# Low parts of twelve weight units made by an adding DMA instead of a subtraction

## The chip, the cores and the metric

The program runs on one core of a Trainium2 chip. The metric is the device time of one execution in microseconds (us), as the median of several runs. The engines are named as the profile names them: PE is the matrix engine (TensorE), PEld its weight loads, DVE is VectorE, ACT is ScalarE, POOL is GpSimd, and SP is the engine that issues most DMAs.

## The reference

Two model blocks run one after the other on a sequence of 512 tokens of width 1024, all in float32. Only the first mixer of the first block is touched:

```python
def even_mixer(h, w_in, sink, w_pool, pool_scale, w_out):
    z = h @ w_in
    q, k, v, u = jnp.split(z, [A_WIDTH, A_WIDTH + A_KV_WIDTH, A_WIDTH + 2 * A_KV_WIDTH], axis=-1)
    q = rope(q.reshape(Bsz, S, A_HEADS, A_HEAD_DIM))      # 8 heads of 64
    k = rope(k.reshape(Bsz, S, A_KV_HEADS, A_HEAD_DIM))
    ya = windowed_gqa(q, k, v, sink)
    yb = multiscale_pool(u, w_pool, pool_scale)           # 4 groups, windows 2, 4, 8, 16
    return jnp.concatenate([ya, yb], axis=-1) @ w_out
```

After it come a squared-ReLU MLP, a second mixer, a second MLP, and a second block. Nothing of them changes.

## The kernel before, in words

Every float32 product is made of three faster ones. An activation or a weight `w` is split into a high part `hi`, which is `w` rounded to the short format that PE multiplies fast, and a low part `lo = w - hi`. For each 128x128 block of weights PE then issues three multiplies of 512 columns, in this order: `hi` of the activation by `wh` (the weight's high part), `hi` by `wl` (its low part), and `lo` by `wh`. In the trace they are `mm<-hi,wh`, `mm<-hi,wl`, `mm<-lo,wh`.

Weights come in units of 128x1024 elements, 512 KB, which are eight such blocks, so 24 multiplies. A unit is loaded by a DMA of SP into a tile `wr`. `copy` (line 572) writes `wh`, on ACT or POOL, whichever the planner expects to be free first, and `tt` (line 586) makes `wl` from `wr` and `wh`, on DVE or POOL by the same rule. There are four buffers each for `wr`, `wh` and `wl`.

The program for all engines is written by a planner that runs when the kernel is built. `_Flow` keeps a clock of its own (`fl.now`), adds a cost for each instruction, and lets tasks go on when they are due. So a changed cost or a changed due time moves the order of the instructions on every engine. Each engine then executes its own list strictly in order and waits at an instruction until what it needs is there. The rule that matters below: the planner puts the multiplies of a unit on PE's list only when `Unit.ready` says that the unit is there, at the planner's clock.

The stage around the change is phase "a", the first mixer. PE's list mixes two sorts of work there. One is the attention of eight heads: score products (`sc`), transposes of the weights of the softmax (`tr`), and the products with the values (`av`), each in turn with maxima (`mx`, `nm`) and low parts (`pl`) on DVE and exponentials (`p<-sc,nm`), scalings (`p<-p,w`), high parts (`ph`) and sums of halves (`cmb`) on ACT. The other sort is filling work that depends on no attention: the projections of `pooling()` from units `ein3` and `ein4` (two each), then the first half of the output projection, units `eout0` and `eout1` (two each). After the attention the second half, `eout2` and `eout3`, follows. These are the last twelve units of the first mixer.

Each of the four projections of `pooling()` feeds a chain, `pool_chain`: `up` is read out of PSUM by DVE, window sums `us` are added up on DVE or POOL (one addition for the first group, four for the last), `pd` is made on DVE, its high part on ACT, its low part `lo<-pd,hi` on DVE or POOL, and then PE multiplies by the unit `wpool`, again as three multiplies.

Of the kernel before, what the change touches and what calls it, by code (L numbers as in the profile page):

```python
# [13 lines left out]
AF = mybir.ActivationFunctionType  # L14
ALU = mybir.AluOpType
# [41 lines left out]
_WT = {}  # L57
# [431 lines left out]
def tile_hybrid(ctx: ExitStack, tc: tile.TileContext, wt, xT, pT, prm_d, cst_d, out):  # L489
    nc = tc.nc  # L490
# [3 lines left out]
    fl = _Flow()  # L494
    go = fl.go
    V, S, G = (_Engine(fl, e, k) for e, k in ((nc.vector, "V"), (nc.scalar, "S"), (nc.gpsimd, "G")))
# [13 lines left out]
    def uid(s):  # L510
        cnt[0] += 1
        return f"{s}{cnt[0]}"
# [44 lines left out]
    def f(ap):  # L557
        return ap.bitcast(F32)
# [12 lines left out]
    def first(*engines):  # L571

        return min(engines, key=lambda e: max(e[0].free, fl.now) + e[1])[0]

    def width(ap):
        n = 1
        for d in ap.shape[1:]:
            n *= d
        return n

    def copy(out, src, scale=None):

        n, ps = width(out), src.space == PSUM
        sc = 1.0 if scale is None else scale
        e = first((S, 0.06 + n / 1090.0), *(() if ps else ((G, 0.07 + n * 0.00117 + fl.gc),)))
        if e is S:
            S.activation(out, src, AF.Copy, scale=sc)
        else:
            G.tensor_scalar(out, src, sc, 1.0, op0=ALU.mult, op1=ALU.mult)

    def tt(op, out, a, b, bias=None):

        n = width(out)
        if PSUM in (a.space, b.space):
            e = V
        else:
            e = first((V, 0.07 + n / 960.0), (G, 0.07 + n * 0.00227 + (fl.gt if bias is None else bias)))
        e.tensor_tensor(out, a, b, op=op)


    NRAW, NSPLIT, AHEAD = 4, 4, 3
    units, order = {}, []

    class Unit:
# [57 lines left out]
        def split(self):  # L662
            while len(self.at) < len(self.parts):
                self.load()
            r = self.raw
            self.hi = wp.tile([P, 1024], F32R, tag="whi", bufs=NSPLIT, name=uid("wh"))
            self.lo = wp.tile([P, 1024], F32R, tag="wlo", bufs=NSPLIT, name=uid("wl"))
            wl["split"] += 1
            wl["due"] -= 1
            for (c0, c1), t in zip(self.parts, self.at):  # L670
                while fl.now < t:
                    yield 0.1
                copy(self.hi[:, c0:c1], r[:, c0:c1])
                yield
                tt(ALU.subtract, self.lo[:, c0:c1], r[:, c0:c1], f(self.hi[:, c0:c1]), fl.gw)
                if c1 == self.n:
                    wl["raw"] -= 1
                yield
                self.ready = c1

        def use(self, n):
# [4 lines left out]
    wl = {"raw": 0, "split": 0, "dma": 0.8, "due": 0}  # L686
# [1729 lines left out]
```

## Time and profile before

| what | value |
|---|---|
| median of three runs | 1477.36 us (1476.55 to 1479.11) |
| the profiled execution | 1479.96 us |
| its span in the profile | 1478.2 us |
| PE busy in that span | 1449.5 us |
| DVE, ACT, POOL busy | 899.0, 649.5, 310.7 us |

The profiled execution is 1.8 us longer than its span, which is what lies before its first and behind its last instruction, and 2.6 us longer than the median of the runs. A share of busy time over the whole span says little about one stage; the stage of the first mixer lies in the first 150 us.

### The profile page before, as it was taken

To read this page: it belongs to the slowest core of one execution; us is meant where nothing else is said; L and a number is where in the kernel's file an instruction comes from. 1 tells how busy PE (TensorE), PEld (TensorE's weight loads), DVE (VectorE), ACT (ScalarE), POOL (GpSimd) and SP (SyncE) were. 2 spreads that over 40 slices of the span, in tenths; PEclk is the share of its full clock that TensorE was granted. 3 is DMA by queue.
4 is the path that set the end of the run, shared out by engine and by line. 5 is a ranking of instruction groups with operands and counts; after the bars stand their busy time and mean duration, and the time that the engine had idled before them with its cause. 6 is when DMAs were issued, how large, how long until landed. Compare 5 with 4: busy or idle time off the path is not lost.

```text
span 1478.2 us, 18891 instructions
## 1 busy us (share of the span) xinstructions
PE 1449.5 (98%) x6789; PEld 1174.4 (79%) x6789; DVE 899.0 (61%) x1410; ACT 649.5 (44%) x1192; POOL 310.7 (21%) x291
## 2 busy tenths in 40 slices
PE   8999999999999999899999999999999999999998
PEld 5777878888888888688888888888787788888787
DVE  7896864655434555977775665657755566536413
ACT  5684432433222347487433434334521576324623
POOL 5451220211102013631120210202110000100332
PEclk9999999999999999999999999999999999999999
DMA  6113588888423454333499999999865223346252
GB/s 212 52 44 99 176 291 272 286 290 280 133 95 100 137 213 158 127 129 128 149 318 330 327 330 330 314 336 323 287 216 195 109 86 115 115 182 214 103 196 89
DMA packets 118317, 291.44 MB, mean 197 GB/s; under 512 B 13136, under 2 KB 14672, under 8 KB 118224
## 3 DMA queue, kind: packets, MB, share of 16 engines
q1 hardware_dynamic: 118080, 289.98, 57.9%
q8 instruction: 53, 0.87, 0.2%
q14 instruction: 40, 0.33, 0.1%
q10 hardware_dynamic: 144, 0.26, 0.1%
HBM read 205.26 MB, written 84.93 MB: 196 GB/s over the span
## 4 chain that ended last, share of the span: by engine, by line
PE 83%; DMA 7%; DVE 5%; issue 1%; ACT 1%; SPq 1%; POOL 0%; DVEq 0%; POOLq 0%; ACTq 0%
PE mm L561 72%; PE sc L561 4%; PE av L561 3%; PE tr L565 3%; DMA kr<-in_wt_dram 3%; DMA wk<-klo 2%; PE tr L561 1%; DMA wk<-khi 1%; DVE wl L363 1%; DMA x<-in_xT_dram 1%; ACT wh L363 1%; DVE klo L363 0%; DVE gz L363 0%; DVE sg L363 0%; DMA pin<-in_pT_dram 0%
## 5 line engine op out<-in xcount | busy, mean ns | idle before, releaser
L561 PE MATMUL mm<-hi,wh 128*128 128x512 f32 (+1 forms) x1276 | 509.4, 399 | 0.8 <-POOL wh L363 0.5
L561 PE MATMUL mm<-hi,wl 128*128 128x512 f32 (+1 forms) x1276 | 501.1, 393 | 4.4 <-DVE wl L363 2.6
L561 PE MATMUL mm<-lo,wh 128*128 128x512 f32 (+1 forms) x1276 | 499.3, 391 | 0.3 <-POOL lo L363 0.3
L561 PEld LDWEIGHTS mm<-lo,wh 128*128 128x128 f32 x1276 | 240.4, 188 | 55.6 <-POOL lo L363 0.8
L561 PEld LDWEIGHTS mm<-hi,wl 128*128 128x128 f32 x1276 | 240.8, 189 | 54.9 <-DVE wl L363 3.6
L561 PEld LDWEIGHTS mm<-hi,wh 128*128 128x128 f32 x1276 | 240.9, 189 | 52.9 <-ACT wh L363 1.5
L363 ACT ACTIVATE khi<-kr 128x512 fp32r<-128x512 f32 x120 | 75.8, 632 | 308.8 <-DMA kr<-in_wt_dram 303.1
L561 PE MATMUL mm<-ul,wh 128*128 128x512 f32 x512 | 201.6, 394 | 1.8 <-DVE ul L363 1.8
L561 PE MATMUL mm<-uh,wh 128*128 128x512 f32 x512 | 201.7, 394 | 0.3 <-ACT uh L363 0.3
L561 PE MATMUL mm<-uh,wl 128*128 128x512 f32 x512 | 201.6, 394 | 0.0
L363 DVE TENSOR_TENSOR wl<-wr,wh 128x1024 fp32r<-128x1024 f32 (+1 forms) x145 | 184.5, 1273 | 6.4 <-ACT wh L363 4.8
L363 DVE TENSOR_TENSOR klo<-kr,khi 128x512 fp32r<-128x512 f32 x150 | 124.3, 830 | 87.7 <-ACT khi L363 77.3
L363 ACT ACTIVATE wh<-wr 128x1024 fp32r<-128x1024 f32 (+1 forms) x147 | 148.8, 1013 | 47.8 <-PE mm L561 34.4
L363 DVE TENSOR_TENSOR x<-x,mm 128x512 f32<-128x512 f32 x112 | 76.8, 686 | 151.0 <-PE mm L561 146.3
L363 POOL TENSOR_TENSOR ma<-ma 128x512 f32<-128x512 f32 x62 | 85.4, 1377 | 282.7 <-ACT uh L363 232.2
L561 PEld LDWEIGHTS mm<-ul,wh 128*128 128x128 f32 x512 | 96.2, 188 | 25.2 <-DVE ul L363 2.9
L561 PEld LDWEIGHTS mm<-uh,wh 128*128 128x128 f32 x512 | 96.1, 188 | 23.1 <-ACT uh L363 0.7
L561 PEld LDWEIGHTS mm<-uh,wl 128*128 128x128 f32 x512 | 96.2, 188 | 22.3
L363 ACT ACTIVATE p<-sc,nm 128x512 f32<-128x512 f32 (+3 forms) x136 | 75.2, 557 | 30.4 <-DVE nm L363 27.3
L363 DVE TENSOR_TENSOR pl<-tr,ph 128x512 fp32r<-128x512 f32 (+2 forms) x108 | 66.5, 623 | 25.4 <-ACT ph L363 24.8
L363 POOL TENSOR_SCALAR khi<-kr 128x512 fp32r<-128x512 f32 x30 | 28.6, 953 | 250.3 <-DMA kr<-in_wt_dram 214.1
L363 DVE SCALAR_TENSOR_TENSOR ma<-mm,rb 128x512 f32<-128x512 f32 x64 | 44.1, 688 | 52.4 <-PE mm L561 52.2
(290 smaller groups left out, 1619.0 us busy)
## 6 DMA issues: line engine op xcount, KB each, us to landing
wr<-in_wt_dram SPq DMA_DIRECT2D x144, 512.0 KB, 5.3
kr<-in_wt_dram SPq DMA_DIRECT2D x150, 256.0 KB, 5.9
wk<-khi SPq DMA_DIRECT2D x150, 256.0 KB, 5.9
wk<-klo SPq DMA_DIRECT2D x150, 256.0 KB, 5.7
wh<-wk SPq DMA_DIRECT2D x74, 512.0 KB, 3.3
wl<-wk SPq DMA_DIRECT2D x74, 512.0 KB, 4.2
x<-xs SPq DMA_DIRECT2D x16, 256.0 KB, 5.1
cst<-in_cst_dram SPq DMA_DIRECT2D x8, 256.0 KB, 5.4
```

Source lines behind the costliest of these rows:

```text
L363: return fn(*a, **k)
L561: PE.matmul(o, l, r, start=start, stop=stop, skip_group_check=True)
L565: PE.transpose(o, i, idn)
```

## The change

For the units named in `ADDED`, all of the twelve, the low part is made in another way. ACT writes the negated, rounded weight into the tile `wl` (the negated high part). `copy` writes `wh` as before. Then POOL issues a DMA that reads the float32 weights from HBM once more and adds them onto what is in `wl`. The subtraction goes away. The planner counts the `wr` buffer as free as soon as the copies are made; it books 1 us of POOL for the issue and 3 us of DMA time, and takes the unit as ready at least 7 us after the issue.

```diff
+    ADDED = ("ein3", "ein4", "eout0", "eout1", "eout2", "eout3")
@@ class Unit, split
-                copy(self.hi[:, c0:c1], r[:, c0:c1])
-                yield
-                tt(ALU.subtract, self.lo[:, c0:c1], r[:, c0:c1], f(self.hi[:, c0:c1]), fl.gw)
-                if c1 == self.n:
-                    wl["raw"] -= 1
-                yield
+                if self.name in ADDED:
+
+                    S.activation(self.lo[:, c0:c1], r[:, c0:c1], AF.Copy, scale=-1.0)
+                    copy(self.hi[:, c0:c1], r[:, c0:c1])
+                    if c1 == self.n:
+                        wl["raw"] -= 1
+                    yield
+                    c = 1024 * self.i
+                    nc.gpsimd.dma_start(self.lo[:, c0:c1], wt[_WT[self.name], :, c + c0:c + c1], accum_op=ALU.add)
+                    G.free = max(G.free, fl.now) + 1.0
+                    wl["dma"] = max(wl["dma"], fl.now) + 3.0
+                    yield max(7.0, wl["dma"] + 4.0 - fl.now)
+                else:
+                    copy(self.hi[:, c0:c1], r[:, c0:c1])
+                    yield
+                    tt(ALU.subtract, self.lo[:, c0:c1], r[:, c0:c1], f(self.hi[:, c0:c1]), fl.gw)
+                    if c1 == self.n:
+                        wl["raw"] -= 1
+                    yield
```

The lists of the engines are the same as before, names of buffers apart, up to the first of these units and again behind the first mixer. In between they differ. On PE, in the middle of the attention, where the fifth head is applied (`av_1019` before, `av_1028` after), multiplies of the last pooling projection stood between the attention's products:

```order
L561 MATMUL av_1019<-ph_997,v_367 128x256
L561 MATMUL av_1019<-pl_998,v_367 128x384
L561 MATMUL mm_970<-hi_173,wh_975 128x512
L561 MATMUL mm_970<-hi_173,wl_976 128x512
L561 MATMUL mm_970<-lo_174,wh_975 128x512
L561 MATMUL mm_970<-hi_189,wh_975 128x512
L561 MATMUL mm_970<-hi_189,wl_976 128x512
L561 MATMUL mm_970<-lo_190,wh_975 128x512
L561 MATMUL mm_970<-hi_196,wh_975 128x512
L561 MATMUL mm_970<-hi_196,wl_976 128x512
```

And at the same place of the attention now:

```order
L561 MATMUL av_1028<-ph_995,v_367 128x384
L561 MATMUL av_1028<-pl_996,v_367 128x384
L565 MATMUL tr_1065<-cst,p_882 128x128
L565 MATMUL tr_1065<-cst,p_904 128x128
L565 MATMUL tr_1065<-cst,p_925 128x128
L565 MATMUL tr_1065<-cst,p_882 128x128
L565 MATMUL tr_1077<-cst,p_904 128x128
L565 MATMUL tr_1077<-cst,p_925 128x128
L565 MATMUL tr_1077<-cst,p_882 128x128
L561 MATMUL av_1028<-ph_1030,v_367 128x256
L561 MATMUL av_1028<-pl_1031,v_367 128x256
```

The multiplies have moved behind this piece of attention, because the planner takes their unit as ready later. Of the multiplies `mm` that stood ahead of the last `av` of the attention, 30 now stand behind it.

On POOL, where the last units of the first half of the output projection are made (`eout1`, then `eout2`), one unit was split by POOL alone and the rest was low parts of activations and a scaling:

```order
L363 TENSOR_TENSOR lo_1279<-pd_1247,hi_1278 128x512
L363 TENSOR_SCALAR wh_1328<-wr_798 128x1024
L363 TENSOR_TENSOR wl_1329<-wr_798,wh_1328 128x1024
L363 TENSOR_TENSOR lo_1382<-ya_1242,hi_1381 128x512
L363 TENSOR_SCALAR p_1254<-p_1254,w_1374 128x256
L363 TENSOR_TENSOR lo_1492<-ya_1417,hi_1491 128x512
```

Now POOL makes every high part and issues every adding DMA:

```order
L363 TENSOR_TENSOR lo_1349<-pd_1340,hi_1348 128x512
L363 TENSOR_SCALAR wh_1388<-wr_549 128x1024
L363 TENSOR_SCALAR wh_1392<-wr_798 128x1024
L682 DMA wl_1389<-in_wt_dram 128x1024
L682 DMA wl_1393<-in_wt_dram 128x1024
L363 TENSOR_SCALAR wh_1457<-wr_1382 128x1024
L682 DMA wl_1458<-in_wt_dram 128x1024
```

The DMA for `wl_1389` stands behind two copies, and so behind what the second copy waits for.

## Rows read from the trace of the kernel before

**Rows 1.** The page, busy time by engine (us, share of the span, instructions).

```profile
PE 1449.5 (98%) x6789; PEld 1174.4 (79%) x6789; DVE 899.0 (61%) x1410; ACT 649.5 (44%) x1192; POOL 310.7 (21%) x291
```

**Rows 2.** Stretches: length, busy PE, PEld, DVE, ACT, POOL, PE clock, DMA share, GB/s.

```profile
73.95:87.43 13.48, 13.48 (x85) 11.57 (x82) 12.83 (x33) 11.34 (x29) 4.75 (x7) 1.00 0.13 41
87.43:100.34 12.91, 12.32 (x74) 10.34 (x73) 11.62 (x30) 11.64 (x29) 6.28 (x8) 1.00 0.12 41
100.34:114.18 13.84, 10.04 (x56) 7.27 (x54) 12.93 (x28) 12.23 (x33) 8.90 (x7) 1.00 0.18 50
```

**Rows 3.** PE's waits from 53.8 to 125 us (total, times, longest).

```profile
PE av L561 <- DVE pl L363: 2.3, 2, 1.9
PE mm L561 <- DVE wl L363: 1.2, 2, 0.6
```

**Rows 4.** Timeline of PE (start, duration, what) at single places of the attention.

```profile
53.77 0.40 PE L561 MATMUL sc<-kh,q 128*128 128x256 f32 x2
...
54.37 0.40 PE L561 MATMUL mm<-hi,wh 128*128 128x512 f32 x1
...
56.45 1.02 PE L561 MATMUL tr<-zs,cst 128*128 128x512 f32 x2
...
67.04 0.34 PE L561 MATMUL sc<-kh,q 128*128 128x384 f32 x1
...
67.51 0.34 PE L561 MATMUL av<-ph,v 128*128 128x384 f32 x1
...
67.86 0.49 PE L565 MATMUL tr<-cst,p 128*128 128x128 f32 x3
68.11 0.48 PE L561 MATMUL mm<-hi,wh 128*128 128x512 f32 x1
68.43 0.40 PE L561 MATMUL mm<-hi,wl 128*128 128x512 f32 x1
...
124.78 0.34 PE L561 MATMUL av<-pl,v 128*128 128x384 f32 x1
...
125.65 0.39 PE L561 MATMUL mm<-hi,wh 128*128 128x512 f32 x1
...
132.62 0.40 PE L561 MATMUL mm<-hi,wh 128*128 128x512 f32 x1
```

**Rows 5.** Timeline of DVE in the attention.

```profile
72.64 0.68 DVE L363 TENSOR_TENSOR up<-mm,rb 128x512 f32<-128x512 f32 x1
...
86.37 0.71 DVE L363 TENSOR_TENSOR us<-up 128x527 f32<-128x527 f32 x1
87.21 1.23 DVE L363 TENSOR_TENSOR wl<-wr,wh 128x1024 fp32r<-128x1024 f32 x1
...
97.24 0.68 DVE L363 TENSOR_TENSOR up<-mm,rb 128x512 f32<-128x512 f32 x1
...
111.13 2.24 DVE L363 TENSOR_TENSOR wl<-wr,wh 128x1024 fp32r<-128x1024 f32 x1 [0.57 <-ACT wh L363]
```

**Rows 6.** Timeline of POOL in the attention.

```profile
46.80 0.62 POOL L363 TENSOR_SCALAR q<-ra 64x512 fp32r<-64x512 f32 x1
...
79.42 1.30 POOL L363 TENSOR_TENSOR lo<-pd,hi 128x512 fp32r<-128x512 f32 x1 [2.70 <-ACT hi L363]
...
107.53 1.30 POOL L363 TENSOR_TENSOR lo<-pd,hi 128x512 fp32r<-128x512 f32 x1
108.80 1.05 POOL L363 TENSOR_SCALAR wh<-wr 128x1024 fp32r<-128x1024 f32 x1
109.93 2.36 POOL L363 TENSOR_TENSOR wl<-wr,wh 128x1024 fp32r<-128x1024 f32 x1
```

**Rows 7.** Timeline of ACT in the attention.

```profile
72.34 1.05 ACT L363 ACTIVATE wh<-wr 128x1024 fp32r<-128x1024 f32 x1
...
110.05 1.05 ACT L363 ACTIVATE wh<-wr 128x1024 fp32r<-128x1024 f32 x1
```

**Rows 8.** Loads of `wr` up to 180 us, issue to landing.

```profile
DMA to landing us min/median/max: 3.5/4.1/7.4
```

## The prediction

> **What bounds the kernel now.** The page comes first: PE is busy for 1449.5 us of 1478.2 [rows 1], so the kernel is as long as PE's work plus PE's waits. The change takes no multiply away. It can only act through PE's waits, and only in the first mixer, since the lists of all engines agree again behind it. So the second view is the busy time by stretch over the attention, where a reader should look for the engine that leaves PE waiting. Up to 87.4 us PE is busy all the time. From there to 100.3 us it is idle for 0.6 us of 12.9, and to 114.2 us for 3.8 us of 13.8, while DVE is busy for 12.9 of those 13.8 and ACT for 12.2 [rows 2]. All three engines are nearly full, and PE waits for the other two. The waits by name say for what: 2.3 us for the low parts of the attention (`pl`) and 1.2 us for the low parts of weights (`wl`), both on DVE [rows 3]. The largest, 1.9 us, is an `av` that waits for a `pl` which stands on DVE behind a `wl` subtraction of 2.24 us [rows 5]. That is what the change takes away.
>
> The idle time does not show all waits, since multiplies that wait for each other also read longer. I count PE's work from its list, with the time from start to start: 0.23 us a multiply `mm` (30 of them take from 125.65 to 132.62 us, 6.97 us), 0.60 and 0.47 us for a score product of either kind with its mask, 0.18 or 0.12 us an `av`, 0.11 us a transpose, up to 1.02 us for the wide one of the rotation [rows 4]. From the first score product that both lists share, at 53.77 us, to the last `av`, at 124.78 us, there are 150 multiplies, 21 score products, 62 `av` and 80 transposes, 64.6 us of work in 71.0 us. So PE's waits in the attention are 6.4 us.
>
> **The change part by part.** *Removed.* Twelve subtractions, eleven on DVE (1.23 us alone, 2.24 us when POOL works on two tiles at the same time [rows 5]) and one on POOL (2.36 us [rows 6]). Seven of the eleven stand ahead of the attention's last `pl`. On DVE's list six window sums of 0.71 us [rows 5] come in for them, and four smaller instructions move behind, so DVE is relieved by 7 x 1.23 - 6 x 0.71 + 4 x 0.68 = 7.1 us. The Trainium skill has the reason of the long ones (SBUF — State Buffer, Who interferes with whom): a DVE instruction with two SBUF inputs contends with a GpSimd instruction that reads SBUF; the 2.24 us against 1.23 us agree with it.
>
> *Added on ACT and POOL.* ACT writes the negated part where it wrote `wh`, at the same price, 1.05 us [rows 7]; besides it gets six scalings from POOL. POOL makes the twelve `wh` (1.05 us each [rows 6]) and issues twelve DMAs. POOL is busy for less than two thirds of any of these stretches [rows 2], so this is hidden, except where something waits in POOL's list behind a DMA.
>
> *Moved on PE.* 30 multiplies go behind the last `av`, 30 x 0.23 = 7.0 us. So the stage ends as late as before only if the attention's last `av` comes 7.0 us earlier, at 117.8 us, that is if PE's waits stay 6.4 us. This is the sum to make: the waits of the new order against 6.4 us.
>
> *The new waits.* Where the attention now runs without filling work, PE comes early to the multiply by `wpool`, which needs the chain of a pooling group. Such a chain took from `up` at 72.64 to the end of `lo` at 80.72 us, 8.1 us, for the second group and from 97.24 to 108.83 us, 11.6 us, for the last one [rows 5, 6]; I take the middle, 9.9 us, for the third. With 0.3 us until `up` starts these are 8.4, 10.2 and 11.9 us, against PE's work from the chain's projection to the multiply that waits: 6.0, 6.5 and 4.8 us by the counted lists. The waits would be 2.4, 3.7 and 7.1 us. The chains get shorter where window sums go from POOL to DVE: by the lists two in the second group, none in the third, three in the last. POOL takes 1.30 us for a subtraction of about as many elements, DVE 0.71 us for a sum [rows 5, 6], so that is 1.2, 0 and 1.8 us. Each chain also had one weight subtraction beside it on DVE; whether it held the chain up the rows don't tell, so I take off half of 1.23 us, 0.6 us each. That leaves 0.6 + 3.1 + 4.7 = 8.4 us, against 6.4 us. This part is +2.0 us. The bounds: no shortening gives 13.2 us (+6.8), and the whole subtraction taken off gives 6.5 us (+0.1).
>
> ACT gives a second sum, and both have to hold. From the `wh` at 72.34 to the one at 110.05 us ACT went through 63 instructions, 0.60 us each [rows 7], or 0.53 us without its waits, as it was busy for 35.2 of 40.2 us [rows 2]. From the same place to the attention's last `cmb`, right behind the last `av`, it now has 81: 48.5 us at its old pace, 42.7 us without a wait, so an end between 115 and 121 us where about 118 us means no change: -3 to +3 us, in the middle nothing. The first sum is the later one, and I keep it.
>
> *The adding DMA.* No row shows one, nor any DMA issued by POOL. Below, it can't be quicker than the quickest load, 3.5 us from issue to landing; the median is 4.1 us [rows 8]. Above, it reads both the weights and the tile, so twice the median, 8.2 us, and POOL may need as long for the issue as for its longest instruction, 2.4 us [rows 6]: 10.6 us. I take the load half as long again, for the second read, and 1.05 us on POOL, as for its copy of as many elements: 7.2 us. What it may take without loss is the room in the lists. For the first unit POOL is done with `q` at 47.4 us [rows 6] and with the copy at 48.5 us; PE has 0.60 + 0.47 + 1.02 + 0.23 us of work from 53.77 us until it needs `wl`, so 56.1 us: a room of 7.6 us. For the units of `ein4` the same reckoning (ACT at 0.53 to 0.60 us for each of the 29 instructions between the two) gives 6 to 8 us; for the first unit behind the attention, whose DMA stands behind two copies, about 7 us. So 7.2 us costs nothing at two places and some 0.3 us at two others: +0.6 us.
>
> The Trainium skill (Collectives: The Full Stack, The bandwidth ceiling) says that a reduce step is half as fast as a copy because the add needs two source reads. By that the moving of the data alone doubles and the fixed part does not, so the DMA would stay under 8.2 us; no run here shows it, and the sum goes by the bounds above.
>
> *Sum.* +2.0 + 0.6 = +2.6 us. The profiled execution's 1479.96 us would become 1482.6; it stands 2.6 us above the median of the runs, so the median becomes 1477.4 + 2.6 = **1480.0 us**. A measurement can tell about 0.2%, 3 us, from no change: this would be read as the same, if only just.
>
> **The rivals.** *The adding DMA is late.* If it takes 10 us, PE waits for `wl` at each of four places (the first unit, both of `ein4`, the first behind the attention) for up to 10 - 7.6 = 2.4 us or more, less what the chains would have made it wait anyway: +6 to +9 us, 1483 to 1487 us. For it: POOL writes nothing like this now, its work stretches beside DVE, and DVE is busy nine tenths of the time [rows 2]. Against it: DMA is nearly idle there, with a share of 0.12 to 0.18 [rows 2]. It decides from about 8 us. The Trainium skill names such a case (SBUF — State Buffer, SBUF: two separate sides): GpSimd can't write descriptors while DVE runs in a mode with both ports. What might be of that kind here is only the `nm` of a single column, so by that rule each DMA would be late by next to nothing.
>
> *DVE sets the pace alone* and is relieved by 7.1 us. Then half or more of PE's 6.4 us of waits go, the DMAs landing in their room: -3.2 to -5 us, 1472 to 1474 us. For it: the longest wait stands behind a `wl` [rows 3, 5]. Against it: ACT was busy for 12.2 us of the same 13.8 [rows 2], and less filling work leaves each wait uncovered.
>
> *It does not act*: the relief and the gaps cancel, within 1.5 us. This is the middle of ACT's sum and lies beside the forecast.
>
> **How the numbers follow.** The forecast with the cancelling case has 0.42. The late DMA has 0.38, as its price is unknown over a range of which the upper third decides. The relief has 0.15. A forecast overshot by longer chains (+3.2 to +6.8) has 0.05. So faster by over 0.2% 0.15, same 0.42, slower 0.43. The likeliest case has 1476 to 1481 us for itself; cases of both signs hold much, so the range of 8 in 10 goes from half of the relief, 1474, to the late DMA's far end, 1488 us.
>
> **What would show it.** In the profile after, DVE should be less busy from 74 to 114 us, by 5 us or more, and the wait of PE for DVE's `wl` should be gone. Filling multiplies should be missing in three gaps of the attention, PE's waits there for `lo` of the pooling chains, `ph` and `pl` together near 8 us, and the last `av` near 120 us. The landing of the adding DMA decides: at 7 us no wait for it of a whole microsecond, at 10 us four of them. I am wrong if the DMA is far from 7 us, if the last `av` comes by 115 us, or if anything behind the first mixer changes.

## The result, and the profile after

The changed kernel takes 1491.6 us (median of four runs, 1490.24 to 1494.04) where the kernel before took 1478.23 us beside it: ratio 1.0091, 95% interval 1.0071 to 1.0111. Run again later beside others it gave 1492.31 us, ratio 1.0089 (1.0074 to 1.0104). It is slower by 0.9%, 13.4 us, where 1480.0 us and at most 1488 us were forecast.

The profiled execution took 1490.64 us with a span of 1488.8 us. The page's busy line answers to [rows 1]: PE's busy time grew by 4.1 us, though it makes the same multiplies, and its idle time by 6.5 us.

```profile
PE 1453.6 (98%) x6789; PEld 1177.1 (79%) x6789; DVE 890.4 (60%) x1404; ACT 653.1 (44%) x1199; POOL 318.8 (21%) x302
```

The stretches answer to [rows 2], with two more behind them (length, then busy PE, PEld, DVE, ACT, POOL, PE clock, DMA share, GB/s). First the two more in the kernel before, then all five now:

```profile
114.18:125.07 10.89, 10.89 (x59) 9.22 (x59) 7.79 (x14) 5.38 (x11) 1.76 (x2) 1.00 0.37 132
125.07:150.00 24.93, 24.93 (x109) 20.18 (x108) 14.58 (x19) 10.15 (x14) 2.17 (x1) 1.00 0.27 85
```

```profile
73.95:87.43 13.48, 10.83 (x54) 8.53 (x53) 10.92 (x30) 10.59 (x30) 4.45 (x6) 0.87 0.36 80
87.43:100.34 12.91, 10.62 (x66) 8.68 (x65) 8.92 (x24) 11.03 (x26) 4.59 (x5) 1.00 0.37 81
100.34:114.18 13.84, 12.36 (x70) 9.85 (x68) 11.50 (x28) 10.69 (x29) 4.00 (x7) 1.00 0.05 7
114.18:125.07 10.89, 8.34 (x34) 6.57 (x35) 7.06 (x13) 8.18 (x17) 7.10 (x7) 0.69 0.42 90
125.07:150.00 24.93, 22.31 (x93) 17.88 (x92) 7.32 (x11) 6.18 (x8) 8.72 (x10) 0.93 0.97 219
```

Two things are to be seen. DVE is less busy in the first three (31.3 us against 37.4 us), as forecast, and PE is nevertheless idle for 2.7, 2.3 and 1.5 us of them and for 2.6 us in each of the last two, 11.6 us in all against 4.4 us before. And the PE clock, 1.00 throughout the attention before, has means of 0.87, 0.69 and 0.93. The clock's own record shows three stretches at 1.2 GHz where the rest is at 2.4 GHz: 81.6 to 85.0, 115.7 to 122.6 and 132.8 to 136.2 us, 13.7 us together; the second execution of the same kernel that was traced (e6 below) has three of the same lengths about 1 us later. The first looks like this in PE's timeline (start, duration, instruction, in brackets the wait and what ended it).

```profile
81.37 0.40 PE L561 MATMUL av<-pl,v 128*128 128x256 f32 x1 [2.31 <-DVE pl L363]
81.60 0.60 PE L561 MATMUL mm<-hi,wh 128*128 128x512 f32 x1
82.00 0.63 PE L561 MATMUL mm<-hi,wl 128*128 128x512 f32 x1
...
85.26 0.39 PE L561 MATMUL mm<-hi,wh 128*128 128x512 f32 x1
85.49 0.39 PE L561 MATMUL mm<-hi,wl 128*128 128x512 f32 x1
```

Behind the wait of 2.31 us the multiplies follow each other every 0.43 us, and from 85.26 us every 0.23 us again. So some of the loss sits in busy time, where no list of waits shows it.

PE's waits from 50 to 160 us by name (total, times, longest) answer to [rows 3].

```profile
PE av L561 <- DVE pl L363: 6.4, 6, 2.3
PE mm L561 <- DMA wl<-in_wt_dram: 2.6, 1, 2.6
PE tr L565 <- ACT p L363: 1.9, 2, 1.0
PE tr L561 <- ACT zs L363: 0.6, 1, 0.6
PE av L561 <- ACT ph L363: 0.5, 1, 0.5
```

The wait for DVE's `wl` is gone, as forecast. The waits for the heads' own `pl`, `p` and `ph` are 8.8 us instead of 2.7 us (before, 2.3 us for `pl` [rows 3] and 0.4 us for `ph`). No wait for `lo` of a pooling chain is among them, and those were what the prediction priced. The last `av` starts here, against 124.78 us in [rows 4]:

```profile
127.09 0.34 PE L561 MATMUL av<-pl,v 128*128 128x384 f32 x1
```

To compare kernels whose beginnings differ by a microsecond, I count from the first score product (44.81 us before, 43.69 us now) to the last `av`, and from there to the sums of the norm that follows the mixer (165.34 us before, 178.69 us now). Both ends before, then now:

```profile
44.81 0.40 PE L561 MATMUL sc<-kh,q 128*128 128x256 f32 x2
...
165.34 0.95 PE L561 MATMUL tr<-onec,sq 128*128 128x1 f32 x8
```

```profile
43.69 0.40 PE L561 MATMUL sc<-kh,q 128*128 128x256 f32 x2
...
178.69 0.95 PE L561 MATMUL tr<-onec,sq 128*128 128x1 f32 x8
```

The first part grew from 79.97 to 83.40 us although 30 multiplies had left it, the second from 40.56 to 51.60 us: 14.5 us together. From the norm on the changed execution is 2.7 us shorter than the profiled execution of before (1310.2 against 1312.8 us), in lists that agree. The other traces spread from 1309.2 to 1316.1 us there (e9, which has no adding DMA, 1312.9 us; e7, with PE's list of before, 1311.4 us); what makes this difference stays open. With the 1.1 us of the beginnings the two profiled executions differ by 10.7 us; 13.4 us is the difference of the medians.

The first part, by the prediction's count: 30 x 0.23 = 7.0 us of work left and it grew by 3.4 us, so PE's lost time in the attention went from 6.4 to 16.8 us (6.4 + 7.0 + 3.4). PE was idle there for 9.6 us instead of 4.4 us; the rest of the lost time lies in busy time. The second: 7.0 us for the multiplies that came in, 2.6 us for a wait, and 1.5 us because the seven multiplies behind that wait took 3.15 us, where 7 x 0.23 = 1.6 us is usual; together 11.1 us. The wait and some of those multiplies:

```profile
133.04 0.80 PE L561 MATMUL mm<-hi,wl 128*128 128x512 f32 x1 [2.62 <-DMA wl<-in_wt_dram]
133.63 0.63 PE L561 MATMUL mm<-lo,wh 128*128 128x512 f32 x1
...
136.19 0.41 PE L561 MATMUL mm<-lo,wh 128*128 128x512 f32 x1
```

The chain of waits (start, length, what) tells where it comes from, read back from 133.04 us.

```profile
114.43 1.27 POOL us L363
...
116.04 0.58 POOL p L363
...
117.14 1.27 POOL lo L363
...
120.42 2.06 POOL wh L363 x2
122.48 1.90 issue
...
124.39 8.60 DMA wl<-in_wt_dram
...
133.04 17.01 PE mm L561 x66
```

The DMA took 8.6 us and had been issued at 124.39 us, because POOL had a window sum of the last pooling group, a scaling, low parts and two copies ahead of it, and then waited 1.91 us for ACT's negated parts. So in the 18.6 us up to this wait's end the chain that PE waited for ran through POOL and the DMA.

### The profile page after: what moved, and what is told of

Read it like the earlier page. It is cut to its first block, busy times and chain, and to the rows that moved or that the text cites. A ratio compares the mean times of both kernels' runs of the same rounds, so it can differ in the third digit from the quotient of the medians.

```text
span 1488.8 us, 18919 instructions
## 1 busy us (share of the span) xinstructions
PE 1453.6 (98%) x6789; PEld 1177.1 (79%) x6789; DVE 890.4 (60%) x1404; ACT 653.1 (44%) x1199; POOL 318.8 (21%) x302
## 4 chain that ended last, share of the span: by engine, by line
PE 82%; DMA 7%; DVE 6%; issue 2%; POOL 2%; ACT 1%; SPq 1%; POOLq 0%; DVEq 0%; ACTq 0%
PE mm L561 71%; DMA kr<-in_wt_dram 5%; PE sc L561 4%; PE tr L565 3%; PE av L561 3%; PE tr L561 1%; DMA x<-in_xT_dram 1%; DMA wl<-in_wt_dram 1%; DMA wr<-in_wt_dram 0%; POOL khi L363 0%; DVE gz L363 0%; DVE sg L363 0%; ACT wh L363 0%; DMA pin<-in_pT_dram 0%; DVE klo L363 0%
## 5 line engine op out<-in xcount | busy, mean ns | idle before, releaser
L363 DVE TENSOR_TENSOR wl<-wr,wh 128x1024 fp32r<-128x1024 f32 (+1 forms) x134 | 167.6, 1251 | 6.7 <-ACT wh L363 5.5
L363 ACT ACTIVATE wh<-wr 128x1024 fp32r<-128x1024 f32 (+1 forms) x136 | 137.2, 1010 | 46.0 <-PE mm L561 34.5
```

The source lines that it names most:

```text
L363: return fn(*a, **k)
```

## The experiments

The two counted parts are as above; "ahead" is the number of filling multiplies ahead of the last `av`. The first four ran beside each other, then e5 to e8, then e9 to e11.

| kernel | median us | ratio to before (95%) | ahead | first sc to last av | last av to norm |
|---|---|---|---|---|---|
| before | 1477.9 to 1479.3 | | 177 | 79.97 | 40.56 |
| changed | 1491.6 | 1.0091 (1.0071 to 1.0111) | 147 | 83.40 | 51.60 |
| e1 order alone | 1495.36 | 1.0111 (1.0089 to 1.0133) | 147 | 88.99 | 47.45 |
| e2 DMA, old order | 1509.4 | 1.0195 (1.0165 to 1.0224) | 177 | 109.39 | 40.44 |
| e3 plain DMA | 1487.35 | 1.0053 (1.0038 to 1.0069) | 147 | 85.53 | 47.26 |
| e4 ready after 4 us | 1497.73 | 1.0126 (1.0109 to 1.0143) | 150 | 92.13 | 48.00 |
| e5 zeros in waits | 1490.92 | 1.0086 (1.0071 to 1.0101) | 147 | 80.86 | 52.45 |
| e6 change again | 1492.31 | 1.0089 (1.0074 to 1.0104) | 147 | 83.84 | 51.75 |
| e7 only eout2, eout3 | 1480.09 | 1.0014 (1.0002 to 1.0026) | 177 | 81.49 | 40.56 |
| e8 only ein3, ein4 | 1486.99 | 1.0062 (1.0046 to 1.0077) | 144 | 79.54 | 52.27 |
| e9 pl first | 1475.67 | 0.9978 (0.9969 to 0.9988) | 177 | 78.55 | 40.56 |
| e10 no window sums | 1488.45 | 1.0074 (1.0061 to 1.0088) | 147 | 78.81 | 53.34 |
| e11 only eout0, eout1 | 1480.83 | 1.0021 (1.0012 to 1.0030) | 159 | 79.49 | 44.69 |

(In the expectations the multiplies are counted to the last but one pair of `av`: 174 and 141 stand for 177 and 147.)

**e1, the order without the DMA.** The planner books as in the changed kernel, but the copy on ACT is only booked and DVE subtracts where the DMA was issued.

```diff
-                    S.activation(self.lo[:, c0:c1], r[:, c0:c1], AF.Copy, scale=-1.0)
+                    S.free = max(S.free, fl.now) + 0.06 + (c1 - c0) / 1090.0
+                    fl.last = max(fl.last, S.free)
...
-                    nc.gpsimd.dma_start(self.lo[:, c0:c1], wt[_WT[self.name], :, c + c0:c + c1], accum_op=ALU.add)
+                    nc.vector.tensor_tensor(self.lo[:, c0:c1], r[:, c0:c1], f(self.hi[:, c0:c1]), op=ALU.subtract)
```

> The order of the changed kernel without its DMA. The planner books what the changed kernel books, so PE's list is the changed kernel's (141 filling multiplies ahead of the attention's last av, 174 before the change), but the low parts of the twelve units are made by a subtraction on DVE, which stands where the DMA was issued; the negated copy on ACT and the DMA are left out. Theory 'order': the loss comes from the list, in which the attention runs for long pieces without filling multiplies, so that its own waits lie open and the granted clock falls to its lower level behind them; then this kernel takes 1487 to 1494 us, the last av comes at 124 us or later and at least two stretches of the lower clock lie between 70 and 150 us. Theory 'DMA': the loss comes from the adding DMA (late landing, POOL held up by its issue, copies doubled on ACT); then it takes 1476 to 1482 us and the clock stays at its upper level. The twelve subtractions on DVE could add up to 15 us of DVE's time where DVE sets the pace, which speaks against reading a time over 1494 us as either.

It is 1.1% slower than before without any adding DMA. The last `av` starts at 133.11 us, and two stretches have the lower clock (85.5 to 88.9 and 119.6 to 129.9 us), as the theory "order" expected. The time is 1.4 us above the 1494 us over which the expectation had it speak for neither theory, since twelve subtractions on DVE can add to it. PE's waits for `pl` are longer than in the changed kernel:

```profile
PE av L561 <- DVE pl L363: 10.2, 6, 2.4
```

So a loss of this size needs no adding DMA. Nor does the work on the other engines explain it: up to the last `av` DVE is busy for 71.5 us, 2.1 us more than before, ACT for 57.1 us and POOL for 30.2 us, 3.9 and 3.7 us less. With nearly the same work in another order, of all lists and not of PE's alone, the first part is 9.0 us longer in spite of the 7.0 us of work that had left PE. Against e1 the changed kernel shows what DVE's relief is worth in this order: 5.6 us up to the last `av` (88.99 to 83.40). Behind it the changed kernel takes 4.2 us longer than e1 (51.60 to 47.45), so most of the relief is gone by the norm.

**e2, the DMA without the order.** The planner books the subtraction as before, and the program holds the negated copy and the DMA instead.

```diff
+                if self.name in ADDED:
+                    nc.scalar.activation(self.lo[:, c0:c1], r[:, c0:c1], AF.Copy, scale=-1.0)
                 copy(self.hi[:, c0:c1], r[:, c0:c1])
                 yield
-                tt(ALU.subtract, self.lo[:, c0:c1], r[:, c0:c1], f(self.hi[:, c0:c1]), fl.gw)
+                if self.name in ADDED:
...
+                    nc.gpsimd.dma_start(self.lo[:, c0:c1], wt[_WT[self.name], :, c + c0:c + c1], accum_op=ALU.add)
```

> The DMA without the new order. The planner books the subtraction as in the kernel before, so PE's list is the list of before (174 filling multiplies ahead of the last av), but in its place ACT writes the negated part and POOL issues the adding DMA. Theory 'order': the filling multiplies hide much of the 7.9 us to landing, the clock stays at its upper level, and the time is 1478 to 1486 us, with waits of PE for wl of 2 to 8 us in sum. Theory 'DMA': the units are used a few us after the copy, so each of the first eight waits 3 us or more; 1495 us or more, with over 15 us of waits for wl in the trace.

```profile
PE mm L561 <- DMA wl<-in_wt_dram: 21.0, 4, 7.3
```

Four waits, the longest 7.3 us, make 21 us, and the kernel is 30 us slower. The theory "order" expected 2 to 8 us of them and fell in this form; what "DMA" expected of this run (over 15 us of waits, 1495 us or more) came. In the order of before the DMA can't stand in the place of the subtraction; it needs a later due time. So the loss has two sides, a DMA that takes long and an order that makes room for it.

**e3, a DMA that writes.** Only `accum_op` is left out.

```diff
-                    nc.gpsimd.dma_start(self.lo[:, c0:c1], wt[_WT[self.name], :, c + c0:c + c1], accum_op=ALU.add)
+                    nc.gpsimd.dma_start(self.lo[:, c0:c1], wt[_WT[self.name], :, c + c0:c + c1])
```

> The changed kernel with a DMA that writes instead of adding (the low part then holds the whole weight; the lists are the changed kernel's). Theory 'DMA': the second read and the addition make the landing late; it falls from 7.9 to below 5.5 us, the one wait for it of 2.6 us goes, and the time falls by 4 us or more, to 1487 us or below. Theory 'order': the landing may fall, but the time stays within 3 us of 1491.6 us, since only one wait was for a DMA.

The DMAs from issue to landing in the changed kernel (with POOL's time for the issue above), and then in e3:

```profile
L682 POOL DMA_DIRECT2D wl<-in_wt_dram x12: 858/882/1131, 47.8 to 157.2; - x12
...
DMA to landing us min/median/max: 5.7/7.9/10.8
```

```profile
DMA to landing us min/median/max: 4.5/5.3/7.0
```

The addition costs 2.6 us of the 7.9 us. Without it the wait for `wl` behind the attention is gone and the second part is 4.3 us shorter, though still 6.7 us longer than before, about the 7.0 us of the multiplies that came in. The first part is not shorter but 2.1 us longer, with 17.1 us at the lower clock instead of 10.2 us. The time falls by some 4 to 5 us, nearly as "DMA" expected (1487.35 us where it said 1487 us or below), and stays 0.5% above before. About a third of the loss is the DMA's length at this one place.

**e4, ready after 4 us.**

```diff
-                    yield max(7.0, wl["dma"] + 4.0 - fl.now)
+                    yield 4.0
```

> The changed kernel with the planner taking a unit as ready 4 us after the issue instead of at least 7. 150 filling multiplies stand ahead of the last av, against 141 and 174, so the order lies between the two. Theory 'order': 1481 to 1489 us, fewer open waits of the attention and less time at the lower clock, for some waits for the DMA. Theory 'DMA': the landing takes 7.9 us, so units listed 4 us after the issue wait up to 4 us each; 1492 to 1505 us.

```profile
PE mm L561 <- DMA wl<-in_wt_dram: 13.6, 5, 4.4
PE av L561 <- DVE pl L363: 3.0, 2, 2.8
```

The waits for `pl` fell by half and five waits for the DMA came instead, 13.6 us. The time is in the range of "DMA" and not of "order": what the shorter due time gives back to the order the landing takes, and more.

**e5, zeros in the waits.** 52 multiplies of a zero matrix stand in PE's list where the changed kernel waits. (Those among the transposes seem to alter the weights of one head; the amount of work is the same.)

```diff
...
+    AV = {20: 10, 28: 6, 38: 3, 50: 2, 51: 2, 52: 4}
+    TR = {63: 8, 67: 6}
...
+    def zeros(o, n):
+        for _ in range(n):
+            PE.matmul(o, zero, mb[:, 128:128 + width(o)], start=False, stop=False, skip_group_check=True)
...
```

> The changed kernel with 52 multiplies of zeros put into PE's list at nine places where its trace shows PE waiting (for pl at 81.4, 96.3, 99.0, 116.4 and 119.1 us, for ph at 117.6, for p at 113.1 and 114.7, for the DMA's wl at 133.0 us), about as many as fit into each wait. They add zero to a sum that is open there; all lists are otherwise the changed kernel's. Theory 'clock': the lower clock behind the waits (81.6 to 85.0, 115.7 to 122.6, 132.8 to 136.2 us, 13.7 us at half the rate) costs time of its own; with PE kept busy these stretches go and the kernel gets 3 to 6 us shorter, 1485 to 1489 us. Theory 'waits alone': what PE waits for comes no earlier, the slow multiplies ran in time that was lost anyway, and the time stays within 2 us of the changed kernel's or rises by a few us where the zeros overrun a wait.

> The changed kernel itself, beside the others on the same chip: 1491.6 us as before, within 2 us, by every theory.

e6 is the changed kernel unedited, for the comparison; its lower clock lies at 82.7 to 86.1, 116.8 to 123.6 and 133.9 to 137.3 us, and the mean granted clock of the changed kernel's eight executions is 0.988 to 0.992, that of 41 of the kernel before 0.991 to 0.996. The stretches of e5 that had the lower clock in the changed kernel:

```profile
73.95:87.43 13.48, 11.94 (x74) 9.68 (x74) 11.98 (x31) 11.01 (x30) 4.50 (x6) 1.00 0.35 80
...
114.18:125.07 10.89, 9.48 (x53) 6.54 (x50) 7.48 (x13) 8.89 (x17) 8.29 (x9) 1.00 0.51 101
125.07:150.00 24.93, 22.40 (x97) 17.03 (x97) 9.04 (x12) 5.25 (x6) 8.60 (x9) 1.00 1.01 239
```

The clock is at its upper level throughout them, and the time is 1490.9 against 1492.3 us, within the spread of either. The first part got 3.0 us shorter, and 0.7 us of that was lost again in the second, where the wait for the DMA stayed at 2.5 us behind 11 zeros. So holding the clock up won about 3 us of the attention, of which 2.3 us are left at the norm and 1.4 us in the medians. "Waits alone" is nearer: the time goes by what PE waits for.

**e7, e8 and e11, the change for some units.** Each names four of the twelve units.

```diff
-    ADDED = ("ein3", "ein4", "eout0", "eout1", "eout2", "eout3")
+    ADDED = ("eout2", "eout3")
```

> The adding DMA only for the two units each of eout2 and eout3, which PE needs behind the attention. PE's list is that of the kernel before up to the last av (174 filling multiplies). Theory 'order': no loss in the attention, 1478 to 1482 us, at most a wait of about 2.6 us for the first unit's DMA. Theory 'DMA': the DMAs cost by themselves; with four of the twelve a third of the loss, 1483 us or more.

> The adding DMA only for the units of ein3 and ein4 (four of the twelve), the subtraction for eout0 to eout3. PE's list is the changed kernel's nearly to the end of the attention (144 filling multiplies ahead of the last av). Theory 'order': most of the loss is there, 1487 to 1493 us, with the lower clock near 82 and 116 us. Theory 'DMA': a third of the loss, 1482 to 1485 us.

> The adding DMA only for the four units of eout0 and eout1. PE's list is that of before up to about 100 us; 159 filling multiplies stand ahead of the last av, against 174 and 141. Theory 'order': half of the shift, so the attention's last 20 us get waits of a few us and the time is 1481 to 1486 us. Theory 'DMA': as for any four units with room for their DMA, 1480 us or less, as with eout2 and eout3.

`ein3` and `ein4` (e8) make 0.62% of the 0.9%, `eout0` and `eout1` (e11) 0.21%, `eout2` and `eout3` (e7) 0.14%. The equal thirds of the theory "DMA" do not show; the loss is the larger the earlier the order starts to differ. "Order" had e7 in its range and e8 and e11 at its lower ends (1486.99 us for 1487, 1480.83 us for 1481). In e8 the second part is long too (52.27 us), without an adding DMA there: 33 multiplies came in (7.6 us), PE waits 1.7 us for a `lo` on DVE, and 3.4 us have the lower clock. The 1.5 us of e7's first part are a stretch of lower clock from 114.9 us on:

```profile
114.18:125.07 10.89, 10.89 (x52) 9.18 (x52) 7.45 (x13) 5.11 (x9) 2.79 (x3) 0.84 0.31 111
```

There PE was busy all the time, and 3.4 us at the lower clock cost 1.5 us. PE's list in e7 is the list of before from end to end, and its waits in the attention are the same (the longest 1.92 us, at 113.37 us); the traced execution of before kept the upper clock behind that wait and this one did not. So a stretch of lower clock can come without a new order, and some of the clock's share in the loss may differ from execution to execution.

**e9, the place of one subtraction.** This is the kernel before with one instruction moved: the subtraction of the second unit of `eout0` is issued behind two `pl` that it stood ahead of.

```diff
...
+                if (self.name, self.i) == ("eout0", 1):
+                    V.free = max(V.free, fl.now) + 0.07 + (c1 - c0) / 960.0
+                    fl.last = max(fl.last, V.free)
+                    later.append((lambda s=self, r=r: nc.vector.tensor_tensor(
+                        s.lo[:, :s.n], r[:, :s.n], f(s.hi[:, :s.n]), op=ALU.subtract)))
+                    left[0] = 2
...
                 yield from split_ps(pt[:, :o], hi[:, :o], lo[:, :o])
+                left[0] -= 1
+                if later and left[0] == 0:
+                    later.pop()()
```

> The kernel before with one DVE instruction moved: the subtraction of the second unit of eout0 (2.24 us at 111.13 us, which two pl of the attention stand behind) is issued behind these two pl. No DMA, no other list changes. Theory 'place': what the change could win in the attention is not DVE's load but what stands ahead of a pl; then the 1.9 us wait of av for pl goes and the time falls by 1 to 2 us, to about 1476.5 us. Theory 'load': DVE has the same work and the next pl is late instead; 1478 us as before, with waits for pl of 2 us or more left.

DVE at that place, which in [rows 5] had the 2.24 us of `wl` at 111.13 us first, and then PE's waits:

```profile
110.64 0.56 DVE L363 TENSOR_TENSOR pl<-tr,ph 128x384 fp32r<-128x384 f32 x1 [0.95 <-ACT ph L363]
...
112.26 0.69 DVE L363 TENSOR_TENSOR pl<-tr,ph 128x512 fp32r<-128x512 f32 x1 [0.30 <-ACT ph L363]
112.87 1.22 DVE L679 TENSOR_TENSOR wl<-wr,wh 128x1024 fp32r<-128x1024 f32 x1
```

```profile
PE mm L561 <- DVE wl L363: 1.2, 2, 0.6
PE av L561 <- ACT ph L363: 0.4, 1, 0.4
PE av L561 <- DVE pl L363: 0.4, 1, 0.4
```

The wait of 1.9 us is gone, `wl` now takes 1.22 us, since it no longer lies beside POOL's (which ends at 111.42 us here), and no other wait grew. At 0.9978 (0.9969 to 0.9988) this kernel beats both. Of the 2.3 us that PE waited for `pl` in the kernel before, 1.9 us came from the place of one instruction. The move also took 1.0 us off DVE there; the run does not part the two.

**e10, no window sums.** The changed kernel, in which the sums and `pd` are booked and not issued.

```diff
...
+            fl.booked_only = True
             tt(ALU.add, nx[:, :n], cur[:, :n], cur[:, s:s + n])
+            fl.booked_only = False
...
-        yield from split_to(a, dd)
+        yield from split_to(a, u)
```

> The changed kernel without the window sums and pd of pool_chain (19 DVE instructions, the rest on POOL); hi and lo are made of up instead, so the pooling's result is another. The planner books them, so PE's list and the other lists stay. Theory 'queue': pl comes late in the stretches without filling multiplies because it stands on DVE behind other chains (mx, nm, pd, ya); PE's waits for pl fall from 6.4 us to 4 us or less and the last av comes 2 to 4 us earlier. Theory 'own chain': a head's own steps (tr, ph, pl, av) are too long for what PE has beside them; the waits stay within 1 us of 6.4 us. In both, the time falls less than the last av moves, since PE then waits longer for the first DMA behind the attention.

```profile
PE mm L564 <- DMA wl<-in_wt_dram: 3.6, 2, 3.0
PE av L564 <- DVE pl L365: 2.9, 5, 1.4
```

The waits for `pl` fell from 6.4 to 2.9 us and the first part by 4.6 us, so "queue" holds; ahead of the last `av` there are 3.4 us at the lower clock instead of 10.2 us, which is in the 4.6 us too. In the changed kernel one sees what stood there: `ph` for the `pl` that PE waits for until 81.37 us was made on ACT by 78.4 us, and DVE then did this, without a pause.

```profile
77.40 0.98 ACT L363 ACTIVATE ph<-tr 128x512 fp32r<-128x512 f32 x2
```

```profile
78.06 0.21 DVE L363 TENSOR_SCALAR nm<-mx,nsink 128x1 f32<-128x1 f32 x1
78.19 0.68 DVE L363 SCALAR_TENSOR_TENSOR pd<-us,up 128x512 f32<-128x512 f32 x1
...
79.20 0.68 DVE L363 TENSOR_TENSOR ya<-av,cmb 64x512 f32<-64x512 f32 x1
79.91 0.56 DVE L363 TENSOR_REDUCE mx<-sc 128x1 f32<-128x384 f32 x1
80.51 0.21 DVE L363 TENSOR_SCALAR nm<-mx,nsink 128x1 f32<-128x1 f32 x1
80.64 1.15 DVE L363 TENSOR_TENSOR pl<-tr,ph 128x512 fp32r<-128x512 f32 x2
```

The `pl` at 80.64 us had been ready for 2.3 us and stood behind `nm`, `mx`, `ya` and the three steps of `pd`. The total fell by less than the first part, 3.2 to 3.9 us, and PE's wait for the first DMA behind the attention got longer.

## Why the prediction was wrong

**Removed: right.** DVE's busy time up to the last `av` fell by 6.1 us (69.4 to 63.3 us in the first part) where 7.1 us was worked out, PE's waits for DVE's `wl` went, and e1 against the changed kernel puts this relief, in the new order, at 5.6 us up to the last `av`.

**Moved on PE: right.** 30 multiplies moved behind the last `av`, and the stage ended later by their 7.0 us because the last `av` did not come 7.0 us earlier but 2.3 us later. The sum to make, waits against 6.4 us, was the right one.

**The new waits: this step failed.** It forecast 8.4 us (bounds 6.5 to 13.2) against 6.4 us, from PE's arrival at the multiply by `wpool`. Measured were 16.8 us, above the upper bound, and none of them at that place. PE, no longer held up by filling multiplies, ran into the heads' own steps: six waits for `pl`, two for `p`, one for `ph`. The step priced one chain and took the others as hidden, though it said itself that less filling work leaves each wait uncovered. e1 shows that such waits come in this order without the DMA and with 2.1 us more work on DVE, and e10 that much of the lateness of the `pl` comes from DVE serving pooling chains and heads in one list. Of the 10.4 us by which the lost time grew, 5.2 us are idle time of PE and about 3 us are the lower clock behind the waits (e5), of which the prediction didn't speak; some 2 us stay without a name. Two of the signs that it named came, DVE's relief and the end of the waits for `wl`, and the listed waits for `pl` and `ph` were 6.9 us where it expected near 8 us with `lo`. So the list of waits alone would have looked nearly right; the last `av`, at 127.09 us instead of near 120 us, did not.

**ACT's second sum** put the end of the attention between 115 and 121 us, at 118 us for no change. ACT's last `cmb` stood at 127.47 us, with ACT busy for 32.3 of the 40.2 us. ACT did not set the pace.

**The adding DMA: nearly right in length, wrong in one place.** 7.2 us were taken and 7.9 us measured, 0.88 us of POOL for the issue where 1.05 us was taken. Of the four places three cost nothing; the first unit behind the attention, put at 7 us of room and 0.3 us, cost 2.6 us and some 1.5 us of lower clock, 4.1 us where the sum had 0.6 us. Two copies and ACT's negated part delayed the issue, two DMAs were issued at once, and that landing took 8.6 us, as the chain of waits shows.

The Trainium skill (Collectives: The Full Stack, The bandwidth ceiling) has the add need two source reads; by it the DMA was estimated to stay under 8.2 us. The median of 7.9 us, 2.6 us above the plain DMA's 5.3 us, agrees, the longest, 10.8 us, does not. How much of the 2.6 us is the second read, no run shows.

**The rivals.** "The adding DMA is late" had the sign and nearly the size, but not the mechanism: of its four waits only one came. e2 shows what it would have been without the late due time. "DVE sets the pace alone" described a real gain that the new order outweighed. The overshoot by longer chains (+3.2 to +6.8 us) was too small and named the wrong waits. Behind the mixer, where the prediction expected no change, the 2.7 us stay open.

Adding up: 10.4 us more lost in the attention, 2.6 us of wait and 1.5 us of clock behind it make the 14.5 us found up to the norm. The 10.4 us are what the count leaves over, so this sum closes by its making; e3, e5 and e10 test its terms. Not settled is how the heads' waits divide between DVE's list and their own steps in each gap: e10 took away 3.5 of 6.4 us at once.

## What to carry to other kernels

When a change makes a unit ready later, count the filling work that leaves a stretch and then go through every wait that this work had covered, the attention's own first, not only the chain that feeds the next new multiply. Before taking work off a nearly full engine, look at which instruction stands ahead of the one that is waited for: moving one subtraction gained 0.2%, while taking twelve away cost 0.9%, by the order and the DMA that came with it. A saving ahead of a DMA that is issued late can be lost again in part at its landing (0.7 of 3.0 us in e5, 1.7 of 4.6 us in e10).

## What the runs showed of the hardware

The granted clock fell to 1.2 GHz behind waits in stretches that had it at 2.4 GHz before, and 52 multiplies of zeros held it up. It fell once without any change of PE's list too (e7, from 114.9 to 118.3 us, behind a wait of 1.92 us that the kernel before passed at 2.4 GHz in its traced execution). The Trainium skill (TensorE: Matmul & The Clock Gate, Terms) puts the price of such time at half of it, which for 13.7 us would be an estimate of 6.8 us. Here it agrees where PE was busy without a pause (1.5 us for 3.4 us in e7), and not where PE waits again soon after: e5 won back 3.0 us in the attention and at most 2.3 us up to the norm.

The adding DMA of 512 KB takes 5.7 to 10.8 us and POOL 0.88 us in the median to issue, a plain one issued by POOL 4.5 to 7.0 us, the loads issued by SP 3.5 to 7.4 us [rows 8].
